# Hybrid decoder on one core: the long convolution's taps leave GpSimd, 17 of one channel tile become products on TensorE

## The chip, the cores and the metric

The kernel runs on one core of one Trainium2 chip. The metric is device time in microseconds (us) of one execution; the median of several runs is compared. The engines of the core work at the same time, each through its own queue in a fixed order: TensorE (PE in the profile, PEld its weight loads), VectorE (DVE), ScalarE (ACT), GpSimd (POOL) and SyncE (SP), which here only issues DMAs. All arithmetic spoken of here is float32, or float32 split into two fp32r parts.

## The reference

Two decoder layers over 256 tokens of width 1024. Each layer is a mixer and a feed-forward part, both followed by a LayerNorm with a scaled residual. The mixer projects the tokens into three groups of heads:

```
qkv  = silu(causal_depthwise_conv(a_q|a_k|a_v, width 4))     # group A, 384 channels
o_a  = gated_delta_rule(q, k, v, decay, beta)                # chunks of 64 tokens
u    = glu_a * sigmoid(glu_b)                                # group B, 256 channels
u    = causal_depthwise_conv(u, width 31) + bias             # the long convolution
o_b  = silu(layer_norm(u))
o_c  = forgetting_attention(f_q, f_k, f_v, log_f)            # group C, 384 channels
x    = layer_norm(alpha * x + (concat(o_a, o_b, o_c) * mix_scale) @ w_out)
```

The long convolution is `u[t, c] = sum over k of w[k, c] * u[t - 30 + k, c]`: 31 taps, each channel for itself. The feed-forward part is a dense SwiGLU in layer 0 and a top-2-of-8 expert SwiGLU in layer 1.

## The kernel before, in words

The program is written in the order mixer 0, dense FFN, mixer 1, experts. In the profile mixer 0 lasts from 0 to about 200 us, the FFN to about 400, mixer 1 to about 610, and the experts take the rest.

Every large product is done with fp32r parts: a piece of weights (1 MB, or 0.5 MB) is loaded by SP (L187), ACT writes its first part (L175, `whi`), DVE the second (L176, `wlo`), and PE makes three products of it (L216, L218 or L220, L223 or L225). In a mixer there are three staging buffers and two for each part, so a load waits until an earlier piece has been split.

A mixer first projects the keys and makes the decay tables. Then comes the chain of the delta rule's triangular inverse (L533, `mm64`): six levels for each of two token blocks. One step of it is a batch of products of 64 x 64 blocks on PE, and then on DVE the updates of X (L564) and Y (L565) and the masked `z` (L551) that the next batch needs. `mm64` lays the products of the two chunks on array rows 0 to 63 and 64 to 127, and writes both into partitions 0 to 63 and 64 to 127 of one PSUM bank.

Beside that chain, and only there to fill the engines, run `values()`, `queries()`, `glu()`, `long_conv()`, and, after the mark "fox" in the inverse, the attention's projections (`fox_values`, `fox_qk`). They are called in that order, followed by the recurrence, the attention's heads, the gates and `conv_norm`, the convolution's LayerNorm. The first two projected tiles behind the keys (`ahead = 2`) go without a wait, the later ones queue up behind the inverse's first product. The order on each engine isn't written by hand: a planner lists the instructions when the program is built, by its own costs and with the program's order as priority, and the engines then follow the list in order.

The long convolution holds channels on the partitions: two channel tiles of 128, 256 tokens each, in `up` with 30 zero columns in front. DVE does the first 20 taps, one instruction for each tap and channel tile (L623 for the first tap with the bias, L626 for the others: `ca = up * tap + ca`). GpSimd does the last 11 taps on both tiles at once (L614, and for each further tap a product into `cq`, L617, and a sum into `cb`, L618). L628 adds `cb` to `ca`.

PSUM has pools by tag: `pj` (2 banks) for projections, `g1` (3) for the delta rule, `f1` (3) for the attention's and the convolution's transposes.

Of the kernel before, what the change touches and what calls it, by code (L numbers as in the profile page):

```python
# [23 lines left out]
POOL_TAPS = 11  # L24
# [15 lines left out]
def tile_hybrid_decoder(ctx: ExitStack, tc: tile.TileContext, x_in, w_in, mix_scale, w_out, gdn_conv_w,  # L40
# [9 lines left out]
    # staging and split buffers for the weights, 8 KB a partition each  # L50
# [3 lines left out]
    # buffers for staging, first and second part  # L54
    WB = (3, 2, 2)

    def more_weights(name):
        """As many buffers again, for a phase that has the room"""
        stack = ctx.enter_context(ExitStack())
        wp["more"] = stack.enter_context(tc.tile_pool(name=name, bufs=1, side="right", reuse_waits="tile"))  # L60
        wp["stack"] = stack
# [26 lines left out]
    # packed [2 chunks x 64 rows, 64 columns]: column minus row within a chunk  # L88
# [8 lines left out]
    # min() operand: +BIG where column >= row, -BIG elsewhere  # L97
    V.tensor_scalar(msk_dt, up64, 2.0 * BIG, -BIG, op0=OP.mult, op1=OP.add)
    # level masks: row and column in the same block of 2b, row in its upper half, column in its lower half
# [22 lines left out]
    # attention mask: BIG where the key comes after the query  # L122
# [36 lines left out]
    def turn_params(l, rows, p):  # L159
        T.transpose(p[:, :R_ROWS], rows, ident[:R_ROWS, :R_ROWS])  # L160
        V.tensor_copy(par[l][:, :R_ROWS], p[:, :R_ROWS])
        # gated norm weight, channel scale and the gate's half in one factor; GLU's half goes into the taps
# [15 lines left out]
    def stage(src, a, b, which=None, into=None):  # L178
        """Loads a DRAM AP of shape [128, a, b], a * b <= 2048."""
# [10 lines left out]
    def parts(staged):  # L190
        """Its (hi, lo) parts"""
# [9 lines left out]
        # in two halves, by columns where one row tile goes with many  # L201
# [10 lines left out]
    def mm3(o, terms, first, last, wide):  # L212
        """o += sum of a.T @ b over the terms (a, b), pairs of fp32r parts; `wide` is the side that holds weights."""
# [14 lines left out]
    def rsqrt_small(dst, src, n, eps, scale, pool):  # L228
        """dst = (src * scale + eps) ** -0.5 on [128, n]"""
        m = V.tensor_scalar(dst, src, scale, eps, op0=OP.mult, op1=OP.add)  # L230
        G.tensor_tensor(dst, dst, mhalf[:, :n], op=OP.pow)
        return m
# [3 lines left out]
    def after(what):  # L236
        """For DVE's work that shall not hold up what has been marked"""
# [4 lines left out]
    def transpose_x(b, mk):  # L242
        """Features of token block b on the partitions, as fp32r parts."""
# [11 lines left out]
    def layer_norm_block(b, y, gam, bet, lp):  # L255
        """xt[:, b] = LN(alpha * xt[:, b] + y), or LN(xt[:, b]) without y"""
# [18 lines left out]
    # =====================================================================================  # L275
    def mixer(l):
# [4 lines left out]
        with ExitStack() as es:  # L281
# [24 lines left out]
            def put_mixed(i, t, src, f):  # L306
                """Channel tile i at tokens t: src (float32, channels on the partitions) times the factor f."""
# [4 lines left out]
            # the projections beside the inverse but the first two queue up behind its start  # L312
# [9 lines left out]
            def proj_tiles(c0, n, use):  # L322
                """Feature-major projection of n 128-column tiles from column c0."""
# [13 lines left out]
            def proj_tok(c0, n, use):  # L337
                """Token-major projection of n (<= 256) columns from c0."""
# [9 lines left out]
            def gated(dst, p):  # L348
                """2 silu(p)"""
# [29 lines left out]
            # softplus of both  # L379
# [12 lines left out]
            # cumulated decay per chunk: by token, of the chunk, by state row  # L392
# [20 lines left out]
            # decay between positions of a chunk, [source, head, target]  # L413
# [15 lines left out]
            def short_conv(g, keep):  # L429
                """2 silu(conv)"""  # L430
# [20 lines left out]
            def tok_tile(cv, t, i, sq=None):  # L451
                """Channel tile i, token-major, and its squares"""
# [12 lines left out]
            def normed(cvs, name, factor, mul=None):  # L465
                """Token-major tiles, the reciprocal norms times `factor` per token and head, these times `mul`,
                and the tokens times all of it with features on the partitions"""
# [30 lines left out]
            with after("normed"):  # L498
                for b in range(NB):
                    # the keys' norm goes with their decay  # L500
# [10 lines left out]
            def in_chunk(b, left, name):  # L511
                """decay times (k of the source, left of the target): [source, head, target] within the chunks"""
# [15 lines left out]
            def mm64(p, lhs, rhs):  # L528
                """per head and chunk: p = lhs.T @ rhs on 64 x 64 blocks"""
# [44 lines left out]
            ca = gp.tile([128, 2, SEQ], F32, name="ca")  # L574
            fv = gp.tile([128, NB, GW], F32, name="fv")
# [32 lines left out]
            def long_conv():  # L608
                cb = gp.tile([128, 2, SEQ], F32, name="cb", tag="th", bufs=1)
                nd = CK - POOL_TAPS  # L610

                def tap(k):
                    return P[:, R_C31 + 2 * k:R_C31 + 2 * k + 2, None].to_broadcast([128, 2, SEQ])
                G.tensor_mul(cb, up[:, :, nd:nd + SEQ], tap(nd))  # L614
                for k in range(nd + 1, CK):
                    q = gp.tile([128, 2, SEQ], F32, name="cq", tag="cq", bufs=1)
                    G.tensor_mul(q, up[:, :, k:k + SEQ], tap(k))  # L617
                    G.tensor_add(cb, cb, q)  # L618
                for k in range(nd):
# [797 lines left out]
```

## Time and profile before

| | |
|---|---|
| time, median of 3 runs | 1678.57 us (1676.71 to 1678.74) |
| span of the profiled execution | 1677.1 us |
| PE busy | 1568.1 us (94%) |
| PE weight loads busy | 1366.0 us (81%) |
| DVE busy | 1385.1 us (83%) |
| ACT busy | 1020.0 us (61%) |
| POOL busy | 120.3 us (7%) |

The profile is of one execution; its span, from the first to the last instruction, is 1677.1 us, within the three runs' own times. A timeline row gives the start, the time from its first start to its last end, the engine, the line in the code, the operation, the tiles out<-in with their shapes, and how many instructions are drawn together (x24); in brackets stands the idle time of the engine before it, and what ended that. Starts can follow each other faster than the durations say, since instructions of one engine overlap in its pipeline. A float32 product shows as two MATMUL instructions, so 24 MATMULs of `mm64` are 12 products. A row of waits gives the line that waited, what it waited for, and the time in total, the count and the longest.

### The profile page before, as it was taken

How to read it: one execution, taken by the hardware profiler on the slowest of the kernel's cores; microseconds unless marked ns; L12 is line 12 of the kernel's file. 1: busy time of each engine (PE TensorE's matmuls, PEld its weight loads, DVE VectorE, ACT ScalarE, POOL GpSimd, SP SyncE). 2: the span in 40 equal slices, each digit the busy share in tenths (PEclk: the TensorE clock that was granted, in tenths of full speed). 3: DMA queues.
4: the chain of work that ended last, by engine and by line, in shares of the span. 5: the costliest groups of instructions: out<-in, count | busy, mean ns of one | idle time of the engine just before them, and what ended most of it. 6: DMA issues, size and time to landing. Idle time of an engine off the chain costs nothing. (4 is left out here: it accounts for less than half of the span.)

```text
span 1677.1 us, 28178 instructions
## 1 busy us (share of the span) xinstructions
PE 1568.1 (94%) x11147; PEld 1366.0 (81%) x11147; DVE 1385.1 (83%) x1860; ACT 1020.0 (61%) x1375; POOL 120.3 (7%) x124
## 2 busy tenths in 40 slices
PE   7979899998797989999999999999999989999995
PEld 6868699997697767888888888888988878888894
DVE  7798855455879888989988889887898988988997
ACT  5314544442523556777777677676787777777783
POOL 5052100000216000000000000000000000000000
PEclk9989999998897979999999999999999999999998
DMA  5333665532313367999999999998999999999992
GB/s 136 110 95 109 226 202 195 183 113 65 98 55 114 132 221 256 341 372 344 350 361 345 319 366 332 339 343 295 324 364 334 345 320 337 359 325 340 341 370 81
DMA packets 274795, 430.03 MB, mean 256 GB/s; under 512 B 11900, under 2 KB 181938, under 8 KB 274656
## 3 DMA queue, kind: packets, MB, share of 16 engines
q1 hardware_dynamic: 272864, 423.81, 73.1%
q0 software_dynamic: 1792, 4.35, 0.9%
q8 instruction: 89, 1.46, 0.4%
q14 instruction: 50, 0.41, 0.1%
HBM read 427.08 MB, written 1.05 MB: 255 GB/s over the span
## 5 line engine op out<-in xcount | busy, mean ns | idle before, releaser
L176 DVE TENSOR_TENSOR wlo<-w,whi 128x1024 fp32r<-128x1024 f32 (+1 forms) x812 | 944.0, 1210 | 127.9 <-ACT whi L175 121.0
L175 ACT ACTIVATE whi<-w 128x1024 fp32r<-128x1024 f32 (+1 forms) x812 | 791.9, 1037 | 260.9 <-PE pj L220 50.1
L216 PE MATMUL t<-whi,x 128*128 128x512 f32 x448 | 179.4, 401 | 0.3 <-DVE x L176 0.3
L218 PE MATMUL t<-whi,x 128*128 128x512 f32 x448 | 176.2, 393 | 0.0
L223 PE MATMUL t<-wlo,x 128*128 128x512 f32 x448 | 124.4, 396 | 0.0
L216 PE MATMUL t<-x,whi 128*128 128x256 f32 x448 | 109.5, 282 | 0.0
L220 PE MATMUL t<-x,whi 128*128 128x256 f32 x448 | 109.4, 282 | 0.0
L216 PE MATMUL pj<-xth,whi 128*128 128x256 f32 x368 | 99.8, 304 | 9.7 <-DVE cv L440 3.7
L216 PEld LDWEIGHTS t<-whi,x 128*128 128x128 f32 x448 | 84.3, 188 | 19.9 <-DVE x L176 0.5
L223 PEld LDWEIGHTS t<-wlo,x 128*128 128x128 f32 x448 | 83.8, 188 | 20.1 <-DVE wlo L176 0.4
L218 PEld LDWEIGHTS t<-whi,x 128*128 128x128 f32 x448 | 84.4, 188 | 18.2
L220 PE MATMUL pj<-xtl,whi 128*128 128x256 f32 x368 | 97.9, 298 | 0.0
L1166 PE MATMUL t<-whi,x 128*128 128x256 f32 x588 | 87.3, 287 | 8.5 <-DVE x L176 3.3
L1168 PE MATMUL t<-wlo,x 128*64 128x256 f32 x672 | 94.6, 282 | 0.0
L1166 PEld LDWEIGHTS t<-whi,x 128*128 128x128 f32 x588 | 78.1, 190 | 14.6 <-DVE h L1247 4.4
L216 PE MATMUL py<-whi,hT 128*128 128x512 f32 x224 | 88.0, 393 | 0.0
L218 PE MATMUL py<-whi,hT 128*128 128x512 f32 x224 | 87.4, 390 | 0.0
L220 PE MATMUL ph<-xtl,whi 128*128 128x256 f32 x352 | 86.4, 283 | 0.0
L216 PE MATMUL ph<-xth,whi 128*128 128x256 f32 x352 | 86.3, 283 | 0.0
L220 PEld LDWEIGHTS t<-x,whi 128*128 128x128 f32 x448 | 84.4, 188 | 0.8
L216 PEld LDWEIGHTS t<-x,whi 128*128 128x128 f32 x448 | 84.4, 188 | 0.8
L216 PEld LDWEIGHTS pj<-xth,whi 128*128 128x128 f32 x368 | 74.5, 203 | 12.2 <-ACT whi L175 7.1
(430 smaller groups left out, 2874.9 us busy)
## 6 DMA issues: line engine op xcount, KB each, us to landing
w<-in_moe_w_dram SPq DMA_DIRECT2D x333, 1024.0 KB, 6.4
w<-in_ffn_w_dram SPq DMA_DIRECT2D x33, 1024.0 KB, 5.3
w<-in_w_in_dram SPq DMA_DIRECT2D x18, 1024.0 KB, 5.7
w<-in_w_out_dram SPq DMA_DIRECT2D x8, 1024.0 KB, 4.9
w<-in_w_in_dram SPq DMA_DIRECT2D x14, 512.0 KB, 3.9
spare<-in_moe_w_dram SPq DMA_DIRECT2D x3, 1024.0 KB, 7.9
xt<-in_x_dram SPq DMA_DIRECT2D x2, 512.0 KB, 4.0
gam<-in_ln_mix_g_dram POOLq DMA_DIRECT2D x2, 512.0 KB, 4.0
```

Of the source, the lines that this page charges most:

```text
L175: S.activation(hi, src, AF.Copy)
L176: return V.tensor_sub(lo, src, hi.bitcast(F32))
L216: T.matmul(o, a[0], b[0], start=first and i == 0, stop=False)
L218: T.matmul(o, a[1], b[0], start=False, stop=False)
L220: T.matmul(o, a[0], b[1], start=False, stop=False)
L223: m = T.matmul(o, a[0], b[1], start=False, stop=last and i == n - 1)
L1166: T.matmul(o, flat(a), b[0], start=first and i == 0, stop=False)
L1168: T.matmul(o[:64], a[:, 0, :], b[1], start=False, stop=False)
```

## The change

- `POOL_TAPS = 11` goes, `PE_TAPS = 17` comes. GpSimd does no tap any more.
- For channel tile 1 the first 17 taps are products on PE. A tap is a diagonal matrix; only its two diagonal blocks of 64 x 64 are stored, in `diag`, 128 partitions x 17 taps x 64. GpSimd makes them with one multiplication of 17 x 64 columns. For each tap two float32 products of 64 rows, 64 columns and 256 tokens add up in one bank of `f1`: one on rows and partitions 0 to 63, one on 64 to 127.
- DVE does all 31 taps of channel tile 0, and the last 14 of tile 1: 45 instructions in place of 40. Then it adds the bank to tile 1 (128 x 256), in place of the sum over both tiles (128 x 512).
- `glu()` is called ahead of `values()` and `queries()`, not behind them.

Comments and docstrings are gone from the new file as well. The diff without these:

```diff
-POOL_TAPS = 11
+PE_TAPS = 17
...
             ca = gp.tile([128, 2, SEQ], F32, name="ca")
+            diag = gp.tile([128, PE_TAPS, 64], F32, name="diag")
+            taps = P[:, R_C31:R_CB].rearrange("p (k i) -> p k i", i=2)[:, :PE_TAPS, 1:2]
+            G.tensor_mul(diag, id64[:, None, :].to_broadcast([128, PE_TAPS, 64]),
+                         taps.to_broadcast([128, PE_TAPS, 64]))
             fv = gp.tile([128, NB, GW], F32, name="fv")
...
             def long_conv():
-                cb = gp.tile([128, 2, SEQ], F32, name="cb", tag="th", bufs=1)
-                nd = CK - POOL_TAPS
-
-                def tap(k):
-                    return P[:, R_C31 + 2 * k:R_C31 + 2 * k + 2, None].to_broadcast([128, 2, SEQ])
-                G.tensor_mul(cb, up[:, :, nd:nd + SEQ], tap(nd))
-                for k in range(nd + 1, CK):
-                    q = gp.tile([128, 2, SEQ], F32, name="cq", tag="cq", bufs=1)
-                    G.tensor_mul(q, up[:, :, k:k + SEQ], tap(k))
-                    G.tensor_add(cb, cb, q)
-                for k in range(nd):
-                    for i in range(2):
+
+                p = f1()
+                for k in range(PE_TAPS):
+                    for h in (slice(0, 64), slice(64, 128)):
+                        T.matmul(p[h, :SEQ], diag[h, k, :], up[h, 1, k:k + SEQ], start=(k == 0),
+                                 stop=(k == PE_TAPS - 1))
+                for k in range(CK):
+                    for i in range(2 if k >= PE_TAPS else 1):
                         c = R_C31 + 2 * k + i
-                        if k == 0:
-                            V.tensor_scalar(ca[:, i, :], up[:, i, 0:SEQ], P[:, c:c + 1],
+                        if k == i * PE_TAPS:
+                            V.tensor_scalar(ca[:, i, :], up[:, i, k:k + SEQ], P[:, c:c + 1],
                                             P[:, R_CB + i:R_CB + i + 1], op0=OP.mult, op1=OP.add)
                         else:
                             V.scalar_tensor_tensor(ca[:, i, :], up[:, i, k:k + SEQ], P[:, c:c + 1], ca[:, i, :],
                                                    op0=OP.mult, op1=OP.add)
-                V.tensor_add(ca, ca, cb)
+                V.tensor_add(ca[:, 1, :], ca[:, 1, :], p[:, :SEQ])
...
             with after("keys' tok"), after("keys"):
+                glu()
                 values()
                 queries()
-                glu()
                 long_conv()
```

## Rows read from the trace of the kernel before

**Rows 1.** The page: busy time of each engine, and two rows of the span in 40 slices of 42 us (busy tenths).

```profile
PE 1568.1 (94%) x11147; PEld 1366.0 (81%) x11147; DVE 1385.1 (83%) x1860; ACT 1020.0 (61%) x1375; POOL 120.3 (7%) x124
...
PE   7979899998797989999999999999999989999995
...
DVE  7798855455879888989988889887898988988997
```

**Rows 2.** Busy time in stretches of the two mixers. The columns are the stretch, its length, busy us and count of PE, PEld, DVE, ACT and POOL, the granted TensorE clock (1.00 is 2.4 GHz, 0.50 is 1.2 GHz), the DMA share and GB/s.

```profile
48.00:96.00 48.00, 46.38 (x766) 44.66 (x767) 37.02 (x68) 12.21 (x23) 4.37 (x4) 1.00 0.30 87
96.00:120.00 24.00, 12.26 (x166) 11.61 (x166) 24.00 (x26) 5.70 (x8) 20.65 (x16) 0.79 0.15 47
498.00:528.00 30.00, 19.23 (x202) 18.55 (x199) 30.00 (x33) 6.60 (x10) 23.11 (x18) 0.73 0.29 92
522.00:528.00 6.00, 6.00 (x50) 5.88 (x49) 6.00 (x10) 0.87 (x2) 0.45 (x1) 0.50 0.52 167
84.00:142.00 58.00, 45.59 (x555) 43.35 (x549) 56.77 (x85) 18.03 (x41) 33.52 (x26) 0.91 0.37 115
489.00:547.00 58.00, 46.92 (x534) 45.26 (x529) 56.22 (x84) 17.73 (x39) 32.94 (x26) 0.85 0.36 113
```

**Rows 3.** What PE waited for: the first row from 84 to 200 us, the second from 480 to 610 us.

```profile
PE g L533 <- DVE z L551: 12.0, 3, 8.1
PE g L533 <- DVE z L551: 11.1, 3, 7.2
```

**Rows 4.** DVE in order of time, in mixer 0.

```profile
83.76 2.04 DVE L626 SCALAR_TENSOR_TENSOR ca<-up,par,ca 128x256 f32<-128x256 f32 x4
...
100.74 0.54 DVE L551 TENSOR_TENSOR z<-g,lvl 128x384 f32<-128x384 f32 x1
...
106.74 2.06 DVE L176 TENSOR_TENSOR wlo<-w,whi 128x1024 fp32r<-128x1024 f32 x1
108.72 4.06 DVE L626 SCALAR_TENSOR_TENSOR ca<-up,par,ca 128x256 f32<-128x256 f32 x3
...
115.44 0.54 DVE L551 TENSOR_TENSOR z<-g,lvl 128x384 f32<-128x384 f32 x1
...
120.49 1.21 DVE L176 TENSOR_TENSOR wlo<-w,whi 128x1024 fp32r<-128x1024 f32 x1
...
124.02 0.41 DVE L662 COPY fv<-f 128x256 f32<-128x256 f32 x1
...
126.89 1.66 DVE L626 SCALAR_TENSOR_TENSOR ca<-up,par,ca 128x256 f32<-128x256 f32 x4
```

**Rows 5.** Line 626 alone (DVE, one tap on one channel tile), its busy time and count in three stretches of mixer 0, before, during and after GpSimd's nine taps in a row.

```profile
83.00:91.00 8.00, 2.42 (x5) 1.00 0.10 26
91.00:118.00 27.00, 19.41 (x17) 0.83 0.30 91
118.00:129.00 11.00, 4.52 (x11) 0.95 0.63 190
```

**Rows 6.** GpSimd in order of time: the reciprocal norms of the keys in mixer 0, one product of a tap, and the norms in mixer 1.

```profile
30.75 3.01 POOL L478 TENSOR_TENSOR rn<-rn,mhalf 128x4 f32<-128x4 f32 x3 [6.99 <-DVE rn L476]
...
95.25 1.11 POOL L617 TENSOR_TENSOR cq<-up,par 128x512 f32<-128x512 f32 x1
...
432.90 1.99 POOL L478 TENSOR_TENSOR rn<-rn,mhalf 128x4 f32<-128x4 f32 x2 [7.83 <-DVE rn L476]
```

**Rows 7.** PE in order of time: batches of the inverse at the full clock and behind a wait, the projection that follows them, and float32 products of 64 rows with 128 and 256 columns.

```profile
62.15 0.91 PE L533 MATMUL g<-Y,z 64*64 64x64 f32 x24
62.90 0.87 PE L533 MATMUL g<-z,Y 64*64 64x64 f32 x24
63.60 0.87 PE L533 MATMUL g<-X,al 64*64 64x64 f32 x24
64.40 0.39 PE L220 MATMUL pj<-xtl,whi 128*128 128x256 f32 x1
64.62 0.28 PE L216 MATMUL pj<-xth,whi 128*128 128x256 f32 x1
...
101.34 1.03 PE L533 MATMUL g<-Y,z 64*64 64x64 f32 x24 [3.60 <-DVE z L551]
...
104.86 0.58 PE L220 MATMUL pj<-xtl,whi 128*128 128x256 f32 x1
...
116.04 1.55 PE L533 MATMUL g<-Y,z 64*64 64x64 f32 x24 [8.14 <-DVE z L551]
...
118.80 0.54 PE L661 MATMUL f<-ident,fvf 128*128 128x128 f32 x2
...
141.78 0.59 PE L695 MATMUL pl<-fk,fq 64*128 64x256 f32 x2
142.30 0.81 PE L519 MATMUL g<-tf,cv 64*64 64x64 f32 x32
...
505.99 1.55 PE L533 MATMUL g<-Y,z 64*64 64x64 f32 x24 [3.57 <-DVE z L551]
...
510.02 0.58 PE L220 MATMUL pj<-xtl,whi 128*128 128x256 f32 x1
```

**Rows 8.** The end of the queries' short convolution on DVE, and the transposes that take up the values on PE.

```profile
70.72 0.43 DVE L444 SCALAR_TENSOR_TENSOR cv<-ct,cv 128x256 f32<-128x256 f32 x1
...
123.66 0.66 PE L455 MATMUL g<-ident,cv 128*128 128x128 f32 x4
```

## The prediction

> **What bounds the kernel now.** I read the page's first two parts first. PE is busy in 94% of the span, DVE in 83%, GpSimd in 7%, and by slices PE stands at 9 nearly everywhere, but falls to 7 in slices 1, 3, 11 and 13 [rows 1]. The experts behind slice 15 leave PE no room, so time is to be had in the mixers, and what a mixer ends earlier, all that follows starts earlier. The chain that ended last covers only the final LayerNorm and says nothing of this change.
>
> Next come the stretches of the mixers. From 96 to 120 us DVE is busy for all of the 24.00 us while PE works for 12.26, at a mean granted clock of 0.79; from 498 to 528 us DVE fills 30.00 and PE works for 19.23 at 0.73. Just before, from 48 to 96 us, it is the other way about: PE 46.38 of 48, DVE 37.02 [rows 2]. The waits name the place: PE's batch of the inverse (L533) waits for `z` (L551) for 12.0 us in three waits in mixer 0, and for 11.1 us in mixer 1 [rows 3].
>
> In DVE's own order one sees why `z` is late. It is a short instruction, 0.54 us, but between the one at 100.74 and the one at 115.44 stand taps and splits, and these have become slow: three taps take 4.06 us, a split of 128x1024 takes 2.06, where four taps took 2.04 before and 1.66 after, and the same split 1.21 after [rows 4]. Line 626 alone gives the ratio: 2.42 / 5 = 0.48 us a tap while GpSimd is idle, 19.41 / 17 = 1.14 us while it does its taps, 4.52 / 11 = 0.41 when it has stopped for the while [rows 5]. So DVE and GpSimd hold each other up when both read from SBUF, DVE falls behind its list, and PE, which has its own list in order, stands still behind a batch that waits for `z`. The bound of that stretch is DVE slowed by GpSimd; around it, it is PE.
>
> **What goes.** GpSimd's taps go, and with them the slow taps and splits. The waits for `z` then cost 12.0 + 11.1 us less [rows 3]. PE also ran slowly behind these waits. Three batches at the full clock take 64.40 - 62.15 = 2.25 us; behind the first long wait three take 104.86 - 101.34 = 3.52, 1.27 more; behind the second wait two take 118.80 - 116.04 = 2.76 in place of 1.50, 1.26 more; in mixer 1 three take 510.02 - 505.99 = 4.03, 1.78 more [rows 7]. From 522 to 528 PE is busy all the time at 0.50, the lower level of 1.2 GHz: 3.0 us of its 6.0 are lost [rows 2]. That is 2.5 us in mixer 0 and 4.8 in mixer 1. Together 12.0 + 2.5 + 11.1 + 4.8 = 30.4 us.
>
> For this DVE must be fast enough without GpSimd. Per mixer it does 45 taps at 0.48 us [rows 5] = 21.6 us, and one addition from PSUM, as the copy of 128x256 from PSUM, 0.41 us [rows 4]: 22.0 us. Before it was some 29.7 us (26.35 for 33 taps in [rows 5], seven more at 0.48), so 7.7 us less with five taps more, and each split that was caught saves 0.85 us [rows 4]. From 84 to 142 us DVE was busy for 56.77 of 58 us [rows 2]; 56.8 - 7.7 - 2 x 0.85 leaves some 47. PE has 45.6 - 2.5 + 9.0 (below) = 52.1 to do there. PE is then the longer one, by 5 us, and that is what I take to be late next.
>
> **What comes.** On PE, per mixer, 17 x 2 = 34 float32 products of 64 rows and 256 columns. The nearest row is the inverse's batch, which has the same two places in the array and the same bank: 36 products of 64 columns in 2.25 us [rows 7], 0.0625 us each, so 0.25 us for 256 columns, and 34 x 0.25 = 8.5 us. The other end is a product of 64 rows and 256 columns whose neighbour does not overlap with it: 142.30 - 141.78 = 0.52 us [rows 7], so 34 x 0.52 = 17.7 us. I take the lower end, since there the layout is the same. Changing between the forms has a price: the first projection behind the batches takes 0.39 us in place of 0.28 [rows 7], 0.11; for some five visits of the taps 0.5 us. So 9.0 us per mixer, 18.0 in all. Nothing hides it: around the stalled stretch PE is full, and where it was stalled it will be full.
>
> The row shows two products of different array rows running at once into one bank. The Trainium skill (TensorEngine Tiling (Array Packing), section Restrictions and Gotchas, on PSUM pressure) says that different row tiles cannot access the same PSUM bank at the same time; by that rule the halves of a tap follow one another, and the sum would be that of the first rival below. The batches at 0.0625 us a product do not bear it out where the partitions differ.
>
> On GpSimd, `diag`: 17 x 64 = 1088 columns against 512 in 1.11 us [rows 6], so 2.4 us, or twice that if DVE holds it up. It needs only the parameters, and GpSimd is idle for 6.99 us before the keys' norms in mixer 0, for 7.83 us in mixer 1 [rows 6]. It costs nothing there; planned behind that gap it would put up to 2.4 us in front of the norms, so at most 5 us in all. I take 0.
>
> The move of `glu()` puts four projected tiles ahead of values and queries. These are not waited for: the queries' convolution ends at 70.72 on DVE, and the first transposes that take up the values come at 123.66 [rows 8], 53 us later, while four tiles delay them by a few us each. The taps can begin earlier, into DVE's idle 48.0 - 37.0 = 11 us between 48 and 96 [rows 2]. SP's loads are the same pieces in another order. The bank of `f1` is held from the first tap on PE to the addition; two are left for the few transposes before the attention's heads. I take 0 for all of this; the idle PE left in that stretch, 48.0 - 46.4 = 1.6 us per mixer, and some of what lies just ahead of it bounds the gain at about 8 us in all.
>
> **The sum.** -30.4 + 18.0 = -12.4 us. Against the profiled span of 1677.1 us that makes 1664.7 us; the median of the runs is 1678.57, 1.5 us above that span, so on its scale 1666.2 us.
>
> **Rivals.**
> - The halves run one after the other (slower). Place: PE, in the taps. Price: 17.7 + 0.5 = 18.2 us per mixer; 36.4 - 30.4 = +6.0, so 1684.6 us. It decides from (15.2 - 0.5) / 34 = 0.43 us a product on. For it: the planner may put projections or the inverse's batches between two halves, and a half alone costs 0.52 us. Against it: the inverse's batches, listed in the same alternating way, overlap [rows 7].
> - The stall stays in part: DVE has 45 taps waiting from early on, and the planner may still list a row of them ahead of a `z`. With half of the waits and of the slow clock left the gain is 15.2 us against 18.0, so 1681.4 us. For it: DVE was full without GpSimd's help too, from 120 on. Against it: 47 us of work in 58, and from 48 to 96, with the same planner, PE hardly waited [rows 2].
> - More than forecast: taps fill DVE's early idle time and PE's, the inverse starts sooner and the gain grows by the 8 us above: 1658 us.
> - That the change doesn't do what it says is excluded: no tap on GpSimd is left, and line 626 is slow only beside those taps [rows 5].
>
> **How the numbers follow.** Forecast 0.60 (its own range, with 7 to 11 us per mixer on PE, and a few us of new waits or of gain, 1661 to 1674 us), halves in turn 0.12, stall half left 0.15, more 0.13. The range of 1655 to 1682 leaves out most of the first rival and the far end of the last. What a measurement can tell from no change is 0.2%, 3.4 us. Faster by more: 0.60 + 0.13 and a third of the second rival, whose price runs from nothing to half, 0.78. The rest of that rival straddles the line: same 0.08, slower 0.14 with the first rival.
>
> **What would show it.** Right: GpSimd empty behind the keys, line 626 at 0.4 to 0.5 us throughout, no wait of PE for `z` above 1 us, clock 1.00 in these stretches, and the taps on PE as 68 instructions in 8 to 9 us per mixer. A pair of halves that takes 1 us speaks for the first rival; waits for `z` of 3 us or more with a fast line 626 for the second. The prediction is wrong if the mixers do not get shorter by some 6 us each, or if the change shows in the FFN or the experts.

## The result, and the profile after

The changed kernel takes 1688.05 us (median of six runs, 1682.87 to 1697.97) against 1678.65 for the kernel before. It is slower by 9.4 us, by the medians a ratio of 1.0056. The ratio on record, taken over the runs, is 1.0064, with a 95% interval of 1.0045 to 1.0083; the ratios and intervals below are of that kind. I had forecast 1666.2 and a range that ended at 1682. The profiled execution has a span of 1686.4 us, 9.3 more than the one before.

The page of the changed kernel: busy times and two rows by slices. They answer to [rows 1].

```profile
PE 1584.4 (94%) x11283; PEld 1372.3 (81%) x11283; DVE 1363.4 (81%) x1870; ACT 1019.9 (60%) x1375; POOL 70.1 (4%) x84
...
PE   5999999998898889999999999999999999999995
...
DVE  5977865455894778888988889887898988898997
```

DVE and POOL are relieved as meant. Counted from 1, slice 3 of PE has gone from 7 to 9, slices 11 and 13 from 7 to 8, but slice 1 has fallen from 7 to 5. The stretches of [rows 2], in the changed kernel:

```profile
48.00:96.00 48.00, 48.00 (x733) 43.55 (x733) 47.79 (x101) 13.35 (x23) 5.33 (x4) 0.99 0.31 90
96.00:120.00 24.00, 22.92 (x357) 21.20 (x354) 16.03 (x28) 6.42 (x12) 0.00 (x0) 1.00 0.30 83
498.00:528.00 30.00, 24.57 (x384) 22.75 (x381) 15.97 (x26) 6.92 (x11) 0.00 (x0) 0.94 0.32 94
84.00:142.00 58.00, 55.28 (x769) 50.73 (x766) 41.64 (x83) 19.57 (x47) 4.62 (x5) 1.00 0.39 119
```

From 96 to 120 us PE works for 22.92 us at the full clock, where it had 12.26 at 0.79. The same microseconds hold other work, though, since the mixer starts later, as is shown below. What PE waited for there, answering to [rows 3]: first row mixer 0 from 48 to 120 us, the others mixer 1 from 451 to 577 us.

```profile
PE f L661 <- ACT fvf L658: 1.1, 1, 1.1
...
PE pj L216 <- ACT fv L656: 3.3, 1, 3.3
PE f L661 <- ACT fvf L658: 1.9, 1, 1.9
PE g L533 <- DVE z L551: 1.4, 3, 1.0
```

The wait for `z` is gone in mixer 0 (12.0 before) and 1.4 in mixer 1 (11.1). A tap on DVE, answering to [rows 5] (count, then min/median/max in ns), and the taps on PE among the inverse's batches:

```profile
L626 DVE SCALAR_TENSOR_TENSOR ca<-up,par,ca x43: 474/482/486, 60.7 to 95.9; 128x256 f32<-128x256 f32 x43
```

```profile
83.78 4.10 PE L617 MATMUL f<-up,diag 64*64 64x256 f32 x34
88.12 0.92 PE L533 MATMUL g<-Y,z 64*64 64x64 f32 x24
```

No tap is slow any more. 34 MATMULs in 4.10 us are 0.12 us each; all 68 keep PE busy for 8.4 us in mixer 0 and 8.6 in mixer 1. So what the change meant to do came about. The question is where the time went, and three points of each mixer answer it: the inverse's first product on PE (L533), the recurrence's last output on DVE (L799), the end of the LayerNorm (the last L272). In the kernel before, then in the changed one:

```profile
44.68 0.36 PE L533 MATMUL g<-id,al 64*64 64x64 f32 x1
...
172.27 0.55 DVE L799 TENSOR_TENSOR oa<-oc,g 128x384 f32<-128x384 f32 x1
...
209.09 1.41 DVE L272 SCALAR_TENSOR_TENSOR xt<-lnr,lnrs,bta 128x512 f32<-128x512 f32 x2
```

```profile
54.00 0.27 PE L533 MATMUL g<-id,al 64*64 64x64 f32 x1
...
176.70 0.55 DVE L799 TENSOR_TENSOR oa<-oc,g 128x384 f32<-128x384 f32 x1
...
212.64 1.41 DVE L272 SCALAR_TENSOR_TENSOR xt<-lnr,lnrs,bta 128x512 f32<-128x512 f32 x2
```

The same points of every profiled execution, as lengths in us. Stretch is from the first product to the last output, ending from there to the LayerNorm's end, FFN from there to the inverse of mixer 1, and rest all that follows mixer 1:

```
                         mixer 0                 FFN    mixer 1         rest     span
                    start  stretch  ending            stretch  ending
before               44.7   128.1    37.7   237.6   128.3    37.7   1063.1   1677.1
after                54.0   123.2    36.8   237.4   125.2    42.5   1067.2   1686.4
e1 wz first          46.5   120.7    37.7   236.3   118.7    36.8   1070.1   1666.9
e2 tail              54.0   123.0    36.8   237.3   125.4    42.5   1063.8   1682.8
e3 all DVE           44.1   125.1    43.2   236.1   123.5    42.9   1067.4   1682.3
e4 glu move only     43.5   126.9    42.1   236.1   129.4    43.2   1063.4   1684.5
e5 wz first, mixer 0 45.1   119.5    37.7   236.8   123.5    42.5   1067.1   1672.1
e6 osq early         53.7   121.3    40.2   237.5   129.3    45.5   1062.6   1690.1
e7 all three orders  45.4   119.7    40.5   236.7   123.3    40.2   1063.0   1668.8
e8 before, wz late   53.5   129.7    37.7   237.4   131.7    42.1   1065.2   1697.3
e9 diag late         50.9   128.7    43.2   236.3   122.4    36.8   1068.6   1686.9
e10 e1, old calls    47.8   123.2    50.8   237.0   124.6    51.4   1067.2   1701.9
e11 all DVE, glu     42.5   121.8    37.1   236.3   113.2    42.1   1062.2   1655.2
e12 e1 and tail      46.5   121.1    37.7   236.4   123.1    36.8   1065.7   1667.4
f1 e1, no products   43.2   118.5    36.8   235.9   108.1    42.1   1062.1   1646.7
f2 8 taps on PE      43.9   125.9    42.1   236.4   118.5    42.1   1062.5   1671.4
f3 after, old calls  55.0   123.6    47.9   237.5   125.4    48.7   1068.0   1706.1
```

The change won 4.9 and 3.1 us in the two stretches, and 0.9 in the first ending. It lost 9.3 at the start, 4.8 in the second ending, and 4.1 behind the mixers. A stretch and its ending are best read together, since the planner's list can move PE work from one to the other: an ending of 36.8 to 37.7 us holds some 150 to 175 MATMULs (PE busy for 30 to 34 us), one of 42.1 to 43.2 some 180 to 205 (35 to 39 us), e10's and f3's of 48 to 51 some 220 to 255. Together mixer 0 went from 165.8 to 160.0 us, mixer 1 from 166.0 to 167.7.

Why the start is late stands on SP's queue. Changed kernel, then the kernel before:

```profile
2.60 0.43 SPq L147 DMA_DIRECT2D small<-in_fox_f_bias_dram  x1
3.08 4.22 SPq L187 DMA_DIRECT2D w<-in_w_in_dram  x3
7.34 2.76 SPq L362 DMA_DIRECT2D wz<-in_w_in_dram  x1
10.14 2.40 SPq L363 DMA_DIRECT2D wz<-in_w_in_dram  x1
```

```profile
3.08 0.43 SPq L362 DMA_DIRECT2D wz<-in_w_in_dram  x1
3.55 0.61 SPq L363 DMA_DIRECT2D wz<-in_w_in_dram  x1
4.20 12.04 SPq L187 DMA_DIRECT2D w<-in_w_in_dram  x4
```

`wz`, the small weights of the decay and the gates, with which the mixer begins, now stands behind three weight pieces. PE waits for its split (before 48 us), and behind it GpSimd has `diag` in front of the decay rows `drow` that the chain needs:

```profile
PE pj L216 <- ACT wzh L175: 9.4, 1, 9.4
```

```profile
30.31 2.04 POOL L577 TENSOR_TENSOR diag<-id,par 128x1088 f32<-128x1088 f32 x1
32.30 1.81 POOL L417 TENSOR_TENSOR drow<-up,gg 128x384 f32<-128x384 f32 x2
41.34 3.01 POOL L478 TENSOR_TENSOR rn<-rn,mhalf 128x4 f32<-128x4 f32 x3 [7.23 <-DVE rn L476]
```

At the far end, four splits in place of two stand on DVE ahead of the product that PE's next transposes (L1273) need. DVE of the changed kernel, and its waits and stretches from 1650 us on (columns as in [rows 2]):

```profile
1647.12 0.67 DVE L1292 TENSOR_TENSOR both<-both,t 64x512 f32<-64x512 f32 x1
1647.72 4.61 DVE L176 TENSOR_TENSOR wlo<-w,whi 128x1024 fp32r<-128x1024 f32 x4
1652.26 0.94 DVE L1309 TENSOR_TENSOR both<-both 64x768 f32<-64x768 f32 x1
```

```profile
PE t L1273 <- DVE both L1309: 1.8, 1, 1.8
```

```profile
1650.00:1656.00 6.00, 4.18 (x17) 2.67 (x15) 6.00 (x8) 3.96 (x6) 0.00 (x0) 0.80 0.00 0
1656.00:1662.00 6.00, 4.89 (x15) 3.28 (x15) 2.66 (x5) 0.60 (x1) 0.00 (x0) 0.64 0.00 0
```

In the kernel before, two splits stood there and PE went on at 1.00:

```profile
1642.21 2.35 DVE L176 TENSOR_TENSOR wlo<-w,whi 128x1024 fp32r<-128x1024 f32 x2
```

```profile
1650.00:1656.00 6.00, 6.00 (x28) 4.37 (x27) 4.14 (x5) 1.13 (x2) 0.00 (x0) 1.00 0.00 0
```

No line of the experts was edited; the planner listed them otherwise.

### The profile page after: what moved, and what is told of

Read it like the earlier page. It is cut to its first block, busy times and chain, and to the rows that moved or that the text cites. A ratio compares the mean times of both kernels' runs of the same rounds, so it can differ in the third digit from the quotient of the medians.

```text
span 1686.4 us, 28430 instructions
## 1 busy us (share of the span) xinstructions
PE 1584.4 (94%) x11283; PEld 1372.3 (81%) x11283; DVE 1363.4 (81%) x1870; ACT 1019.9 (60%) x1375; POOL 70.1 (4%) x84
## 3 DMA queue, kind: packets, MB, share of 16 engines
q8 instruction: 90, 1.47, 0.4%
## 5 line engine op out<-in xcount | busy, mean ns | idle before, releaser
L175 ACT ACTIVATE whi<-w 128x1024 fp32r<-128x1024 f32 (+1 forms) x812 | 791.5, 1037 | 240.9 <-PE py L218 43.2
```

Of the source, the lines that this page charges most:

```text
L175: S.activation(hi, src, AF.Copy)
```

## The experiments

**e1: `wz` first.** The projections' loads may be issued only behind `wz`'s.

```diff
+            wzd = []
             def columns(c0, n):
-                return load(W[:, :, c0:c0 + n], 8, n)
+                with tc.issue_after(wzd[0]) if wzd else nullcontext():
+                    st = stage(W[:, :, c0:c0 + n], 8, n)
+                return parts(st)
...
-            nc.sync.dma_start(wz[0][:, :, 12:], W[:, :, C_FF:C_FF + H])
+            wzd.append(nc.sync.dma_start(wz[0][:, :, 12:], W[:, :, C_FF:C_FF + H]).ins)
```

> The kernel after, with one order forced: the projections' weight pieces may be issued on SP only behind the two loads of wz. Theory A (late start): of the 9.3 us that the changed kernel lost, 5.3 are in the mixers, and they come from wz's loads standing behind three weight pieces in mixer 0. Then wzh is split at 8 to 9 us as in the kernel before (17.2 in the changed one), the inverse's first batch starts at 44 to 48 us (44.7 before, 54.0 changed), the mixer's LayerNorm comes 5 to 9 us earlier than the changed kernel's 206.0, and the time is 1679 to 1684 us, as the end of the experts (3.9 us) is not touched. Theory B (the taps' price on PE is the loss, the late start only uses up slack): the start is early but the LayerNorm of mixer 0 stays within 2 us of 206, time 1686 to 1689.

Measured: 1665.56 us, 0.9918 of the kernel before (0.9902 to 0.9935). That is 13 us below the range expected. The inverse starts at 46.5 us. Its SP queue and GpSimd:

```profile
3.08 0.43 SPq L366 DMA_DIRECT2D wz<-in_w_in_dram  x1
...
22.37 1.82 POOL L421 TENSOR_TENSOR drow<-up,gg 128x384 f32<-128x384 f32 x2
24.16 2.02 POOL L581 TENSOR_TENSOR diag<-id,par 128x1088 f32<-128x1088 f32 x1
34.04 3.01 POOL L482 TENSOR_TENSOR rn<-rn,mhalf 128x4 f32<-128x4 f32 x3 [7.86 <-DVE rn L480]
```

With `wz` in time `drow` comes first, and `diag` lies in GpSimd's idle time. Theory B falls: the LayerNorm of mixer 0 ends 9.1 us earlier than in the changed kernel. The gain of 22.5 us is more than the start's 7.5: mixer 1 is shorter too.

**e5: the same in mixer 0 alone**, and **e8: the kernel before with `wz` late** (three pieces of mixer 0 staged ahead of `wz`'s loads).

```diff
-                with tc.issue_after(wzd[0]) if wzd else nullcontext():
+                with tc.issue_after(wzd[0]) if wzd and l == 0 else nullcontext():
```

> The kernel of e1 with the forced order in mixer 0 alone; mixer 1 is as the planner lists it. e1 gained 22.5 us over the changed kernel, more than its late start of 9 us explains: its mixer 1 alone became 11.7 us shorter. Theory A1 (wz's late load is a loss of mixer 0 only, and mixer 1's gain in e1 comes from the forced order there, by another listing): mixer 0 ends as in e1, mixer 1's LayerNorm comes about 407 to 412 us after mixer 0's as in the changed kernel (405.1), and the time is 1674 to 1680. Theory A2 (with mixer 0 in order the planner lists mixer 1 well too): 1664 to 1668. The activations' list of this kernel has osq of mixer 1 behind the last gate, as in the changed kernel, which speaks for A1.

```diff
...
+            if l == 0:
+                for c0, n in ((C_K, 256), (C_K + 256, 128), (C_V, 256)):
+                    early_w[c0] = stage(W[:, :, c0:c0 + n], 8, n)
+            with after("st") if l == 0 else nullcontext():
+                nc.sync.dma_start(wz[0][:, :, :12], W[:, :, C_DEC:C_DEC + 12])
...
```

> The kernel before, with three weight pieces of mixer 0 put on SP ahead of the two loads of wz: the order of the changed kernel, with all taps as before. Theory A: this alone makes the start late. wzh is split at 17 us, the inverse's first batch starts at 50 to 54 us (44.7 before), mixer 0's LayerNorm 3 to 8 us later than before's 202.5, time 1682 to 1688. Rival (the late start is hidden: PE takes up the key projections first, and the chain makes up for it): LayerNorm within 2 us, time 1677 to 1681.

e5 took 1675.51 us (0.9978 to 0.9998), e8 1695.42 (1.0078 to 1.0115). In both directions the late `wz` moves the start by 9 us (54.0 to 45.1, and 44.7 to 53.5), and the whole by more: 12.5 and 17.7 us, each against the kernel that it was made from; for e8 I had expected 1682 to 1688. The rest is in stretches and endings of a list made anew. e5 gives A1: mixer 1 stays as in the changed kernel (ending 42.5), so the rest of e1's gain comes from the forced order there. `wz` stands behind weight pieces in mixer 1 of the kernel before as well, and e1's start there is no earlier (236.3 against 236.8 in e5); what the other listing gains, I did not separate.

**e9: `diag` behind the keys' products** on GpSimd, `wz` still late.

```diff
-                    G.tensor_mul(n, kt[:, b], bc(fe[:, b]))
+                    marks["kd"] = G.tensor_mul(n, kt[:, b], bc(fe[:, b]))
...
+            with after("kd"):
+                G.tensor_mul(diag, id64[:, None, :].to_broadcast([128, PE_TAPS, 64]),
...
```

> The kernel after, with diag put behind the keys' products on GpSimd's list; wz stays late. In the changed kernel the decay rows (drow) stand behind diag, and the chain of mixer 0 is 8.3 us late at the first key transposes but 9.6 at the keys' decay products. Theory: diag costs up to 2.0 us of that chain (its own duration) since it stands between the parameters and drow. Then the keys' decay products come at 43.9 to 44.8 us (46.0 changed, 36.4 before) and mixer 0's LayerNorm 1 to 2 us earlier: 1684 to 1688. Rival (drow waits for wz's gates anyway, and diag lies in that wait): within 0.5 us at that point.

1684.38 us (1.0022 to 1.005), within the range expected, but not by the way expected. The inverse starts 3.1 us earlier (50.9), so `diag` did cost the chain about what it takes (2.04 us), and a little more:

```profile
29.64 1.78 POOL L417 TENSOR_TENSOR drow<-up,gg 128x384 f32<-128x384 f32 x2
38.37 3.01 POOL L478 TENSOR_TENSOR rn<-rn,mhalf 128x4 f32<-128x4 f32 x3 [6.95 <-DVE rn L476]
```

Two things go with it in the changed kernel. It stands in front of `drow` on GpSimd, and while it runs DVE hardly moves on. The DVE instruction that falls into it in the changed kernel, the one in e1, and the same as e1's in f1, which has no `diag` (there beside `drow`):

```profile
30.09 3.34 DVE L444 SCALAR_TENSOR_TENSOR cv<-ct,cv 128x256 f32<-128x256 f32 x1 [0.64 <-ACT ct L443]
```

```profile
23.63 2.58 DVE L406 TENSOR_TENSOR egd<-gcs 128x12 f32<-128x12 f32 x1
```

```profile
23.12 0.65 DVE L406 TENSOR_TENSOR egd<-gcs 128x12 f32<-128x12 f32 x1
```

The median of L444 in that mixer is 0.42 us. In f2, where `diag` has 8 taps and takes 1.06 us, an L444 beside it takes 1.47. So this is the slowing of [rows 5] once more, with `diag` in the place of GpSimd's taps, and e1 pays it too: f1 starts the inverse at 43.2 us, 3.3 before e1. How much of these 3.3 us is `diag`, beyond the 1.9 that one instruction takes longer, is not separated.

But mixer 0 of e9 ends 8.8 us later, not earlier: its ending went from 36.8 to 43.2 and mixer 1's from 42.5 to 36.8. The good and the bad ending have changed places.

**e2: the end of the experts**, and **e12: e1 with the same edit**. The second-last piece's split goes behind `both`, the last one's behind `hT`.

```diff
...
-                            hi, lo = load(jb.rows(moe_w2)[:, 2 * fs:2 * fs + 2, :], 2, D)
+                            st = stage(jb.rows(moe_w2)[:, 2 * fs:2 * fs + 2, :], 2, D)
+                            with nullcontext() if now or i == 0 else after(("both", "sT")[i - 1]):
+                                hi, lo = parts(st)
...
```

> The kernel after, with one order forced at the very end of the experts: the splits of the last two w2 pieces stand behind the product of both (L1309 of the changed kernel) and the parts of hT on DVE. Theory D: the last 3.9 us of the loss are made there, since four splits in place of two stand before that product, PE waits 1.8 us for it and runs at 0.64 of its clock for the next 6 us. Then PE's wait at L1273 goes below 0.5 us, the clock stays at 1.00 to the last product, and the time is 3 to 4 us under the changed kernel's: 1684 to 1685. Rival (the end is late because the loads or the tokens are late): the wait stays, time 1687 to 1689.

> e1 with the end of the experts mended as in e2. The end took 20.2 us from the 75th last product in the kernel before, 24.7 in e1, 20.3 in e2. If the places are independent: 1665.6 - 4.4 = 1661 us (1660 to 1663). Rival (e1's end is late for another reason): 1664 to 1667.

e2 took 1681.74 us (1.0004 to 1.0026), 6 less than the changed kernel's median and 2 below the time expected, with two splits ahead of the product, no wait at L1273 and the clock at 1.00:

```profile
1647.76 2.35 DVE L176 TENSOR_TENSOR wlo<-w,whi 128x1024 fp32r<-128x1024 f32 x2
1650.03 0.95 DVE L1311 TENSOR_TENSOR both<-both 64x768 f32<-64x768 f32 x1
```

```profile
1650.00:1656.00 6.00, 4.62 (x22) 2.81 (x21) 6.00 (x9) 3.84 (x6) 0.00 (x0) 1.00 0.00 0
1656.00:1662.00 6.00, 6.00 (x27) 4.34 (x26) 4.22 (x7) 1.42 (x3) 0.00 (x0) 1.00 0.00 0
```

Theory D is shown; the rest shrank by 3.4 us, as the table has it, and what is left of the 6 lies within the changed kernel's own scatter. e12 took 1664.00 (0.989 to 0.9923), only 1.6 less than e1 and not clear of the scatter of either, and missed its 1661. Its rest is 4.4 us shorter than e1's, but the profiled execution lost as much in mixer 1's stretch, with a mixer that was listed in the same order. From 536 to 560 us, first e1, then e12:

```profile
536.00:560.00 24.00, 22.03 (x310) 18.95 (x305) 21.16 (x60) 10.07 (x30) 1.32 (x1) 1.00 0.08 22
```

```profile
536.00:560.00 24.00, 23.04 (x283) 20.02 (x277) 18.38 (x58) 10.07 (x32) 1.32 (x1) 0.79 0.07 27
```

At 0.79 of the clock PE loses, by estimate, 0.21 x 23 = 4.8 us, and the stretch is 4.4 longer: the difference is the granted clock. The two profiled executions took 3 and 5 us more than the medians of their kernels.

**e6: the recurrence's squares early** on ACT, and **e7: e1, e2 and e6 together**.

```diff
                     OA.append(o)
+                    sq = gp.tile([128, H, HD], F32, name="osq", tag="sc", bufs=4)
+                    S.activation(sq, o, AF.Square)
...
+                    rsqrt_small(n, n, H, NORM_EPS, 1.0 / HD, gp)
+                    ON.append(n)
...
```

> The kernel after, with the squares of the recurrence's output (osq on ACT, its sum on DVE and power on GpSimd) written directly behind the recurrence, so that ACT's list has them ahead of the attention heads' last activations; wz is late as in the changed kernel. In the changed kernel 8.0 us pass in mixer 1 from the last output of the recurrence to its osq on ACT (4.2 in the kernel before), and 17.4 to the gated output (12.2 before). Theory E (ACT's list costs mixer 1 its gain): osq starts within 4 us of the output, the gated output comes 12 us behind it, mixer 1 gets 4 to 6 us shorter; the end of the experts is listed as in the kernel before here, 3 to 4 us more: 1678 to 1682. Rival (the heads' chain on PE ends late, and the squares only wait for nothing): the gated output stays 16 us or more behind, time 1683 to 1686.

> The changed kernel with all three orders mended: wz's loads first in both mixers, osq directly behind the recurrence, and the splits at the end of the experts behind the product of both. If the three losses are separate places, it is e1's 1665.6 less 3 to 4 us at the end of the experts and 0 to 1 us from osq, which e1 has in good order already: 1661 to 1663. If they are not (the planner lists the rest anew each time), it can come out anywhere from 1660 to 1672.

e6 took 1686.17 us (1.0036 to 1.0069), e7 1667.81 (0.9907 to 0.9951). Theory E falls: the squares moved, to 0.2 us behind the last output in mixer 1, and both endings became longer (40.2 and 45.5). So the squares are not what the ending waits for. e7 is not better than e1 either: its rest is short (1063.0), its endings are long (40.5 and 40.2). These four endings do not follow the count of MATMULs given above (they hold some 150, 200, 160 and 165), so what makes them long stays open, and so does why the planner leaves more or less work for an ending.

**The parts alone: e4, e3, e11, e10, f3.** e4 moves only `glu()` in the kernel before. e3 does all 62 taps on DVE, with the old calls; e11 is e3 with `glu()` first. e10 is e1 with the old calls, f3 the changed kernel with them. The two edits:

```diff
-                values()
-                queries()
-                glu()
+                glu()
+                values()
+                queries()
```

```diff
...
-                for k in range(nd):
+                for k in range(CK):
                     for i in range(2):
...
-                V.tensor_add(ca, ca, cb)
```

> The kernel before with only the call of glu moved to the front; the taps on GpSimd and DVE as before. Theory C (the move of glu makes wz late and costs the 5 us): time 1683 to 1687. Theory A: wz's loads come first here, since it is the plan with the taps on PE that puts them back; the start is that of before (inverse's first batch at 44 to 47 us). The taps begin earlier, beside a GpSimd that slows them as before, so the slow taps only move: 1673 to 1681 us.

> The kernel before with all 62 taps on DVE: no tap on GpSimd, none on PE, no diag, the call order of before. It tells what the removal of GpSimd's taps is worth without PE's price. Theory A: wz's loads come first, so the start is that of before; taps cost 0.48 us each, 62 x 0.48 = 29.8 us of DVE against 29.7 before, the splits beside them are no longer slow, and PE's wait for z shrinks from 12 to 4 to 8 us a mixer: 1668 to 1676 us, with the end of the experts 4 us late by the same order as in the changed kernel (so 1672 to 1680 in all). Theory B: PE has 8.1 us less a mixer than in the changed kernel, 1688 - 16 = 1672. Rival: DVE stays the bound of that stretch, since its work is the same; the wait for z stays at 10 us or more and the time at 1676 to 1682.

> All 62 taps on DVE as in e3, but with glu called first; no taps on PE, none on GpSimd; wz is first and the end of the experts is listed as before. Against e1 it tells what the 17 taps on PE are worth once GpSimd's taps are gone. DVE has 17 taps x 0.48 = 8.2 us more a mixer than in e1, PE 8.1 us less. If PE is the longer engine of the stretch (as I forecast), the stretch gets 8 us shorter than e1's or at least not longer: 1650 to 1666. Rival (DVE in its order is what sets the stretch, as e3 showed with 123.5 to 125 us from the inverse's first product to the last output, against 119 in e1): 1668 to 1678.

> e1 with the call order of before (values, queries, glu): taps on PE and DVE, wz first, glu not moved. It tells whether the move of glu is part of the gain. My prediction has it at nothing in itself but as what lets the taps begin in DVE's idle time between 48 and 96 us. If so, the taps begin at 84 us as before, DVE is full from 84 to 120, PE waits for z for 4 to 8 us a mixer, and the time is 5 to 10 us over e1's: 1671 to 1676. Rival (the move is worth nothing, since DVE is no longer slowed): within 3 us of e1, 1663 to 1669.

> The changed kernel with only the call of glu put back to its place behind the queries; wz is late as in the changed kernel. e10 against e1 says that the move is worth 40 us where wz is first. If that holds here: 1700 or more (1695 to 1715). If the move's worth and the late start share one cause, it stays near 1688 to 1695.

Of these five, e11 and f3 came out as expected. e3 (1685.9) and e10 (1705.5) lie above every range given for them. e4 (1686.7) has theory C's time but not its mechanism: `wz` is in time and the inverse starts at 43.5 us. Medians in us, with the interval of the ratio to the kernel before:

```
                      values, queries, glu             glu, values, queries
taps on GpSimd+DVE    1678.5  (the kernel before)      1686.72  e4   1.0036 to 1.007
all 62 on DVE         1685.86  e3  1.0032 to 1.0066    1656.50  e11  0.985 to 0.9883
17 on PE, wz first    1705.48  e10 1.0145 to 1.0179    1665.56  e1   0.9902 to 0.9935
17 on PE, wz late     1707.71  f3  1.0157 to 1.0194    1688.05  the changed kernel
```

The move of `glu()` costs 8 us beside GpSimd's taps, and gains 29, 40 and 20 us without them. Waits and stretches of mixer 0 say why: e10's wait for `z`, then two of its stretches, 96 to 120 us and its ending, then the same two of e1:

```profile
PE g L537 <- DVE z L555: 9.5, 3, 8.9
```

```profile
96.00:120.00 24.00, 15.05 (x216) 11.83 (x213) 21.01 (x47) 2.00 (x2) 0.00 (x0) 0.79 0.27 84
...
171.00:222.00 51.00, 42.28 (x242) 34.58 (x240) 38.37 (x79) 26.15 (x46) 6.93 (x9) 0.94 0.59 188
```

```profile
96.00:120.00 24.00, 22.19 (x354) 20.86 (x349) 13.24 (x22) 7.04 (x12) 0.00 (x0) 1.00 0.53 161
...
167.00:205.00 38.00, 31.74 (x161) 24.94 (x160) 30.61 (x59) 20.15 (x32) 6.92 (x9) 0.95 0.74 250
```

With the old calls the taps come to DVE in a lump behind the queries (in e10 from 86 us on, 28 of the 45 between 104 and 120), and `z` is late by 9.5 us without any tap on GpSimd beside it. PE work that was not done by then is done in the ending: 42.3 us of PE in place of 31.7, 242 MATMULs in place of 161. Stretch and ending of mixer 0 together are 15.6 us longer than e1's; what they lost beyond the wait, part of it at 0.79 of the clock, is not separated. With `glu` first the taps spread over DVE from 50 to 60 us on. In e4 they spread as well, but beside GpSimd's: a tap takes up to 1.50 us, and PE waits 6.7 us for `z` and 5.9 for the short convolutions.

**f1: e1 without the products on PE**, and **f2: 8 taps on PE** (`PE_TAPS = 8`, `wz` first by the planner's own list).

```diff
...
-                p = f1()
-                for k in range(PE_TAPS):
-                    for h in (slice(0, 64), slice(64, 128)):
-                        T.matmul(p[h, :SEQ], diag[h, k, :], up[h, 1, k:k + SEQ], start=(k == 0),
-                                 stop=(k == PE_TAPS - 1))
...
-                V.tensor_add(ca[:, 1, :], ca[:, 1, :], p[:, :SEQ])
```

> e1 without diag, without the 34 products a mixer on PE and without the addition of their sum; the 17 taps of the second channel tile are left out of the result, DVE does its 45 taps as in e1. Theory P (PE is the engine that the mixer waits for, so each product on it is paid in full): 2 x 8.1 us less than e1, and 4 us less at the end of the experts, which is listed as in the kernel before: 1643 to 1650, some 8 us below e11, which does 17 taps more on DVE. Theory Q (the products fill time in which PE would wait): within 5 us of e12's 1664, so 1659 to 1666. If it lands on e11's 1656.5, the 17 taps cost nothing on DVE and the whole price is PE's.

> The kernel after with 8 taps of the second channel tile on PE in place of 17; the planner lists wz first here by itself, and the end of the experts as in the kernel before. Theory P: 8/17 of the price, 2 x 3.8 us over e11, 1658 to 1664. Theory Q (only the listing differs): no such order, anywhere from 1650 to 1675.

f1 took 1648.98 us (0.9812 to 0.9844), f2 1673.09 (0.9944 to 0.9972). f1 has the end of the experts in good order, so by the medians it is held against e12: 1664.0 - 1649.0 = 15.0 us, near the 17.0 that the products keep PE busy for. That is the number of theory P, but the table does not put it all where the products are. f1 starts 3.3 us before e1 and e12, where no product stands yet; that leaves 11.7. And the two mixers of e1 and f1, stretch and ending together, take 313.9 and 305.5 us: 8.4 us for 17.0 us of products, 3.1 in mixer 0 and 5.3 in mixer 1. In mixer 0's stretch PE is idle for 2.9 us more without the products than with them, so there they filled waits in part. That each product is paid in full is not shown.

On DVE the same 17 taps cost e11 less f1: 7.5 us by the medians, and 8.7 in the two mixers (314.2 us) for 16.4 us of work. So in the mixers the taps cost about as much on DVE as on PE, though one profiled execution of each can't tell differences below the 4.4 us that e1 and e12 differ by: in the two stretches e11's clock was 0.94 and 0.97, e1's 0.99 and 1.00. e11's lead over e1 in the profiled spans, 11.7 us, is 4.0 at the start and 7.9 behind the mixers.

f2, over both e11 and e1 and above the 1658 to 1664 of theory P, follows no count of products: its first stretch is 125.9 us, and its endings, 42.1 twice, hold some 180 and 195 MATMULs where e1's hold some 160.

## Why the prediction was wrong

- **What goes: right.** The waits for `z` went from 12.0 and 11.1 us to nothing and 1.4; the clock from 96 to 120 us rose from 0.79 to 1.00; a tap takes 0.48 us. I had called waits for `z` above 1 us a sign against me; the 1.4 is three waits, 1.0 the longest. The clock from 498 to 528 us came to 0.94, not to 1.00.
- **The time of the products on PE: right; "nothing hides it": not borne out.** 8.5 us a mixer forecast, 8.4 and 8.6 measured. But without them the two mixers of f1 are only 8.4 us shorter than e1's, and by the medians at most 11.7 us can be theirs, not 17.0. A half takes 0.24 us beside its partner where one alone takes 0.52 [rows 7]. By the rule of the Trainium skill that I weighed (TensorEngine Tiling (Array Packing), Restrictions and Gotchas) the halves would have followed one another in the bank; this trace does not agree, and the first rival falls with it.
- **PE late next: right by the busy times.** From 84 to 142 us PE is busy for 55.3 us and DVE for 41.6, where I had 52 and 47, in a mixer that starts 9.3 us later. Yet e11, which takes the 17 taps from PE and gives them to DVE, has mixers no shorter than e1's.
- **The stretch itself** gained 4.9 and 3.1 us in the changed kernel, where I had 15.2 - 9.0 = 6.2 a mixer; in e1 it gained 7.4 and 9.6. In mixer 1 part of it was given back in new waits for the attention's values on ACT (`fv`, `fvf`), 3.3 + 1.9 us. With the endings mixer 0 got 5.8 us shorter and mixer 1 1.7 longer, and I had named as a sign against me that the mixers do not get shorter by some 6 us each. The second rival, `z` late again, did not happen.
- **"SP's loads are the same pieces in another order ... I take 0 for all of this": here it failed.** The list put `wz` behind three pieces, and that was worth 9 us at the start (e1, e5, and e8 the other way round). I had looked only at what values and queries wait for, not at what else stands in SP's queue. And it is not the move of `glu` that does it: e4 and e11 have the move and start at 43.5 and 42.5 us.
- **The move of `glu` at nothing: wrong in the other direction.** It is worth 20 us inside the change (f3). My gain of 30.4 needed it, and I had counted that gain as GpSimd's alone: with the old calls and no tap on GpSimd PE still waits 9.5 us for `z` (e10).
- **`diag` "costs nothing": wrong, by 3.1 us** in the changed kernel (e9), and by some 2 us in e1. I had named the place, GpSimd's idle time before the norms, but `diag` can stand in front of `drow` as well, and I had not asked what it does to DVE, though [rows 5] show DVE slow beside GpSimd. In e1 it lies in GpSimd's idle time and still stretches an instruction of DVE from 0.65 to 2.58 us.
- **Behind the mixers nothing was expected, and 4.1 us were lost**, 3.4 of them by one order on DVE (e2). Neither this nor the second ending (4.8 us) could be read from the diff; why the planner made the second ending so stays open.

e1 comes out at 1665.6 us against my 1666.2, but that is luck, a sum of terms that I did not have: stretches better than forecast, and an end of the experts that is worse.

## What to carry to other kernels

Where a planner writes the lists, a change is the edit and a new list for the whole program; ask first for the small loads at the start of each queue, and hold them in place by an explicit order when the list moves them. Before work goes to an engine that is already the longer one, try whether relieving the contention and starting that work earlier makes room where it was: all 62 taps on DVE with `glu` first take 1656.5 us (e11), 1.3% less than the kernel before and better than any version here that computes all taps. Before a difference is put down as the price of a piece of work, see whether it lies where that work is: e11's lead over e1 does not lie in the mixers. And measure two parts of a change together and apart: taking the taps off GpSimd and moving `glu()` each cost 7 to 8 us alone (e3, e4), and gain 22 us together (e11).

## What the runs showed that I had not expected

- The changed kernel's runs scatter with the granted clock: the fastest of six took 1682.87 us at a mean of 0.977, the slowest 1697.97 at 0.961. The kernel before, in as many runs, keeps within 3 us. In e1 and e12 one and the same list of mixer 1 differs by 4.4 us between two profiled executions, and 24 us at 0.79 of the clock in one of them account for it. What makes the clock fall in one execution and not in the other is not shown.
- The order of splits at the end of the experts cost 3.4 us, with PE waits of 1.8 and 1.1: behind them PE ran at 0.80 and 0.64 for 12 us.
- `diag`, one GpSimd instruction of 2 us, stretched a DVE instruction beside it in each mixer of the changed kernel and of e1: 3.34 us for one of 0.42 (changed kernel, mixer 0), 2.58 for one of 0.65 (e1, mixer 0), 1.76 for one of 0.16 (both, mixer 1).
- Three pieces queued ahead of `wz` at 3.08 us held PE up for 9.4 us (0.9 in e1), though the two loads are issued only 4.3 and 6.6 us later than before.
